# Turning the softmax tiles of a two-layer encoder: sixteen SBUF-to-SBUF transfers in place of a trip through DRAM

## The chip, the cores and the metric

The kernel runs on one core of a Trainium2 chip. The metric is the device time of one execution in microseconds (us), the median of several runs. A profiled execution is one more run, with every instruction recorded.

## The reference

Two transformer layers over 256 rows of 2048 numbers in float32, 16 heads of 128.

```python
# layer 1
u = rms_norm(h, a_norm_g);  q, k, v, fz = split(u @ a_w_in)      # 2048 x (3*2048 + 16)
q, k = rms_norm per head
logf = log_sigmoid(fz + a_b_f);  c = cumsum(logf)
s = q k^T * scale + c[query] - c[key];  causal;  p = softmax(s);  o = p v
h = h + o @ a_w_out
h = h + (relu(rms_norm(h) @ w1) ** 2) @ w2                       # 2048 -> 8192 -> 2048
# shared keys and values, then layer 2
k, v = split(rms_norm(h, kv_norm_g) @ kv_w);  k = rms_norm per head
q = rms_norm per head of rms_norm(h, b_norm_g) @ b_w_q
s = q k^T * scale + bias by distance;  chunks of 64 see themselves and the 8 before;  p = softmax(s);  o = p v
h = h + o @ b_w_out
h = h + the same MLP with its own weights
```

What the change touches is p: for each of the 16 heads and both layers, the softmax probabilities have to be transposed (turned) before the product with v.

## The kernel before

All matrix products are made on TensorE to float32 accuracy from two rounded halves: a tile of weights is split into `hi` (ScalarE, L323) and `lo` (VectorE, L324), activations likewise, and three products hi*hi, hi*lo, lo*hi are summed in PSUM (L592, L594, L596). Many weight blocks also go through a scheme of seven products in place of eight, for which sums of weight blocks are needed (T1 to T4); `make` (L970) forms them on VectorE, and `put` (L980) by a transfer from POOL's queue that adds to its destination. Tiles named `raw`, `zraw`, `R`, `w`, `wT`, `wB` are weights: loaded by `load` (L299) or `bring` (L942) on SP's queue, with four `raw` buffers.

Between two weight tiles `run_fill` works off one or two steps of a list, `fill`; `add_fill` puts small work there, numbered by step. So the attention of one group of four heads runs in between the weight products of the next: `attend` places, from a table, the four steps of `softmax` for each head, then the transfers that turn the probabilities, and some steps later `values` (the product with v, L766 and L767). The order on TensorE, VectorE, ScalarE and SP's queue is the order in which the code is written (`keep_order`); on POOL it is kept for computing alone, and its transfers are placed by the scheduler.

A tile of probabilities, 128 queries by 384 (128 keys for the first 128 queries, 256 for the second), is turned in two moves. VectorE transposes each 32x32 block where it stands (`blocks32`, L440, from `pr` to `z`). Then the blocks must change places: block row i and block column j swap. Both helpers below do that second move. `carry` writes the tile to DRAM whole (`rows`, L450) and, one step later, reads it back in four transfers that take the columns (`columns`, L456). `hop` sends each of the sixteen blocks of 32 partitions straight from SBUF to SBUF (L466): eight from SP's queue, eight from POOL's. In the kernel before, `hop` serves some tiles of the MLP (`turn_hidden`, where a table entry is negative; 32 x 256 numbers a block) and `carry` all others. `z`, `pr` and `pT` of the softmax are slices of one buffer, `pbuf`, so the profile calls all three `pbuf`. There are three rooms for z and four for pT.

POOL also takes the power -0.5 for the norms of the heads (`norm`, L668), for which ScalarE (L674) waits, and prepares the attention's bias (L912 to L917, L1243, L1245).

Of the kernel before, what the change touches and what calls it, by code (L numbers as in the profile page):

```python
# [99 lines left out]
def trunk(ctx: ExitStack, tc: tile.TileContext, xT, xr, gs, hg, bf, wgate, w_in, w_oa, w1a, w1fa, w1sa, w2fa, w2sa,  # L100
# [336 lines left out]
    def blocks32(src, z, b):  # L437
        n = src.shape[1] // P
        nb = z.shape[1] // (n * P)
        V.transpose(z.rearrange("p (j n b c) -> p b n j c", j=4, n=n, b=nb)[:, b],  # L440
                    src.rearrange("p (n j c) -> p n j c", n=n, j=4))

    def carry(z, dst, wait=1, reader=SY):
        w = z.shape[1]
        n = w // 4
        box = []

        def rows():
            box.append(dram.tile([P, w], F32, name="turn", tag=f"turn{w}", bufs=4))
            SY.dma_start(box[0], z)  # L450

        def columns():
            s = box[0].rearrange("(i a) f -> a i f", i=4)
            d = dst.rearrange("p (i f) -> p i f", i=4)
            for j in range(4):
                reader.dma_start(d[32 * j : 32 * j + 32], s[:, :, j * n : (j + 1) * n])  # L456

        return [[rows]] + [[]] * wait + [[columns], [], []]

    def hop(z, dst):  # L460
        n = z.shape[1] // 4

        def go():
            for i in range(4):
                for j in range(4):
                    (G if i % 2 else SY).dma_start(dst[32 * j : 32 * j + 32, i * n : (i + 1) * n], z[32 * i : 32 * i + 32, j * n : (j + 1) * n])  # L466

        return [[go], [], [], [], []]
# [257 lines left out]
    def softmax(st, g, a, q, k, bias, cq):  # L726
        s = ps_o.tile([P, 512], F32, name="po", tag="po")
        TE.matmul(s[:, 0:P], q[:, a, 0:P], k[:, a, 0], start=True, stop=True)  # L728
        TE.matmul(s[:, P : 3 * P], q[:, a, P:T], k[:, a], start=True, stop=True)  # L729
        yield  # L730
        t = wk.tile([P, 3 * P], F32, name="t", tag="wk")
        pr = rooms("pr")
        row = sm.tile([P, 3 * NB], F32, name="row")
        nm, su, rs = (row[:, i * NB : i * NB + NB] for i in range(3))
        halves = ((0, slice(0, P)), (1, slice(P, 3 * P)))
        for b, c in halves:
            if cq is not None:
                V.scalar_tensor_tensor(t[:, c], s[:, c], cq[:, b, g * GH + a : g * GH + a + 1], bias[:, a, c],
                                       op0=ALU.add, op1=ALU.add)
                V.tensor_reduce(nm[:, b : b + 1], t[:, c], axis=AX.X, op=ALU.max, negate=True)  # L740
            else:
                V.tensor_tensor_reduce(out=t[:, c], in0=s[:, c], in1=bias[:, a, c], scale=-1.0, scalar=-3.0 * NEG,
                                       op0=ALU.add, op1=ALU.min, accum_out=nm[:, b : b + 1])
        yield
        for b, c in halves:
            S.activation(pr[:, c], t[:, c], AF.Exp, bias=nm[:, b : b + 1], scale=1.0 if cq is not None else -1.0,
                         accum_out=su[:, b : b + 1])
        yield
        V.reciprocal(rs, su)
        for b, c in halves:  # L750
            V.tensor_scalar(pr[:, c], pr[:, c], rs[:, b : b + 1], None, op0=ALU.mult)
        z = rooms("z")
        blocks32(pr, z, 0)
        st["pT"] = rooms("pT")
        st["carry"] = carry(z, st["pT"], 0)
        yield

    served = set()
# [14 lines left out]
    def attend(g, q, k, v, cq, o, make_bias):  # L773
        st = [{} for _ in range(GH)]
        box = {}
        k4 = k.rearrange("p (i a b c) -> p a b i c", i=4, a=GH, b=NB)
        *at, far = TABLES["ATA" if cq else "ATB"][g]
        items = [[] for _ in range(at[-1] + far + 1)]
        step = steps(lambda: make_bias(g, box))
        for i in (5, 8, 9) if cq and g == 0 else (3, 6, 7):  # L780
            items[i].append(step)
        for a in range(GH):
            step = steps(lambda a=a: softmax(st[a], g, a, q(), k4, box["b"], cq() if cq else None))
            for i in range(4):
                items[at[a] + i].append(step)
            items[at[a] + 3].append(lambda a=a: add_fill(st[a]["carry"]))
            items[at[a] + far].append(lambda a=a: values(st[a], a, v, o, g * GH + a))
        return items
# [589 lines left out]
```

## Time and profile before

| what | before |
|---|---|
| median of three runs | 2051.86 us (2051.32 to 2054.9) |
| profiled execution | 2049.66 us, span 2047.9 us |
| TensorE busy | 2041.1 us |
| VectorE, ScalarE, POOL busy | 1783.5, 1403.7, 245.0 us |
| bytes moved by DMA | 557.78 MB, 272 GB/s |
| granted TensorE clock | 0.999 |

The span runs from the first instruction to the last. PE is TensorE, PEld its weight loads, DVE VectorE, ACT ScalarE, SP the engine that only issues transfers. A time behind an engine is the union of its instructions' times. `out<-in` names the tiles that an instruction writes and reads, L and a number the line of the kernel.

### The profile page before, as it was taken

To read this page: it belongs to the slowest core of one execution; us is meant where nothing else is said; L and a number is where in the kernel's file an instruction comes from. 1 tells how busy PE (TensorE), PEld (TensorE's weight loads), DVE (VectorE), ACT (ScalarE), POOL (GpSimd) and SP (SyncE) were. 2 spreads that over 40 slices of the span, in tenths; PEclk is the share of its full clock that TensorE was granted. 3 is DMA by queue.
4 is the path that set the end of the run, shared out by engine and by line. 5 is a ranking of instruction groups with operands and counts; after the bars stand their busy time and mean duration, and the time that the engine had idled before them with its cause. 6 is when DMAs were issued, how large, how long until landed. Compare 5 with 4: busy or idle time off the path is not lost.

```text
span 2047.9 us, 27097 instructions
## 1 busy us (share of the span) xinstructions
PE 2041.1 (100%) x9062; PEld 1688.5 (82%) x9062; DVE 1783.5 (87%) x2065; ACT 1403.7 (69%) x1805; POOL 245.0 (12%) x351
## 2 busy tenths in 40 slices
PE   9999999999999999999999999999999999999999
PEld 7888888888888888888888888888888888888887
DVE  7788888998898899899988778888988998988996
ACT  7766666677677677677778666667766676776764
POOL 1111110011111102101012111001101111111020
PEclk9999999999999999999999999999999999999999
DMA  8898888998888898898879888888988888888984
GB/s 322 265 298 272 266 280 243 309 278 272 282 262 281 272 293 272 247 292 273 260 242 311 275 254 287 255 264 284 291 291 265 266 270 284 266 284 261 299 259 147
DMA packets 175309, 557.78 MB, mean 272 GB/s; under 512 B 40624, under 2 KB 69184, under 8 KB 152640
## 3 DMA queue, kind: packets, MB, share of 16 engines
q1 hardware_dynamic: 154112, 464.99, 63.9%
q0 software_dynamic: 20768, 90.75, 22.5%
q8 instruction: 71, 1.16, 0.2%
q14 instruction: 70, 0.57, 0.1%
q10 hardware_dynamic: 288, 0.30, 0.1%
HBM read 516.07 MB, written 27.29 MB: 265 GB/s over the span
## 4 chain that ended last, share of the span: by engine, by line
PE 98%; DVE 1%; ACT 1%; issue 0%; DMA 0%; DVEq 0%; ACTq 0%
PE acc L596 23%; PE acc L592 23%; PE acc L594 23%; PE s L592 9%; PE s L594 9%; PE s L596 9%; PE po L729 1%; PE po L766 1%; DVE lo L324 0%; PE po L767 0%; PE po L728 0%; ACT hi L323 0%; DMA gsb<-in_gs 0%; PE pg L868 0%; DVE s L995 0%
## 5 line engine op out<-in xcount | busy, mean ns | idle before, releaser
L324 DVE TENSOR_TENSOR lo<-raw,hi 128x1024 fp32r<-128x1024 f32 (+1 forms) x409 | 493.5, 1211 | 81.5 <-ACT hi L323 77.1
L323 ACT ACTIVATE hi<-raw 128x1024 fp32r<-128x1024 f32 (+1 forms) x409 | 429.5, 1054 | 194.0 <-PE acc L594 123.4
L592 PE MATMUL acc<-hi,act 128*128 128x512 f32 x1774 | 496.3, 393 | 0.7 <-ACT hi L323 0.7
L596 PE MATMUL acc<-lo,act 128*128 128x512 f32 x1774 | 491.1, 390 | 0.7 <-DVE lo L324 0.6
L594 PE MATMUL acc<-hi,act 128*128 128x512 f32 x1774 | 490.7, 389 | 0.0
L596 PEld LDWEIGHTS acc<-lo,act 128*128 128x128 f32 x1774 | 332.5, 188 | 72.1 <-DVE lo L324 3.1
L594 PEld LDWEIGHTS acc<-hi,act 128*128 128x128 f32 x1774 | 333.0, 188 | 70.1 <-DVE act L383 0.5
L592 PEld LDWEIGHTS acc<-hi,act 128*128 128x128 f32 x1774 | 331.2, 188 | 69.6 <-ACT hi L323 2.1
L323 ACT ACTIVATE hi<-w 128x1024 fp32r<-128x1024 f32 x254 | 267.0, 1058 | 124.0 <-PE acc L594 82.7
L324 DVE TENSOR_TENSOR lo<-wT,hi 128x1024 fp32r<-128x1024 f32 x220 | 267.2, 1221 | 66.1 <-ACT hi L323 62.2
L324 DVE TENSOR_TENSOR lo<-w,hi 128x1024 fp32r<-128x1024 f32 x254 | 305.3, 1217 | 14.0 <-ACT hi L323 12.3
L323 ACT ACTIVATE hi<-wT 128x1024 fp32r<-128x1024 f32 x220 | 232.1, 1059 | 102.1 <-PE acc L594 48.5
L592 PE MATMUL s<-hi,act 128*128 128x512 f32 x530 | 146.3, 391 | 0.0
L596 PE MATMUL s<-lo,act 128*128 128x512 f32 x530 | 145.0, 389 | 0.0
L594 PE MATMUL s<-hi,act 128*128 128x512 f32 x530 | 144.8, 388 | 0.0
L466 POOL DMA_DIRECT2D q<-z x192 | 95.7, 510 | 255.1 <-DVE z L440 211.0
L596 PEld LDWEIGHTS s<-lo,act 128*128 128x128 f32 x530 | 99.2, 188 | 20.8 <-DVE lo L324 0.5
L594 PEld LDWEIGHTS s<-hi,act 128*128 128x128 f32 x530 | 99.4, 188 | 20.6
L592 PEld LDWEIGHTS s<-hi,act 128*128 128x128 f32 x530 | 99.1, 188 | 20.2
L592 PE MATMUL s<-hi,S 128*128 128x512 f32 x288 | 89.6, 392 | 0.0
L596 PE MATMUL s<-lo,S 128*128 128x512 f32 x288 | 88.8, 390 | 0.0
L594 PE MATMUL s<-hi,S 128*128 128x512 f32 x288 | 88.7, 389 | 0.0
(217 smaller groups left out, 2284.4 us busy)
## 6 DMA issues: line engine op xcount, KB each, us to landing
raw<-in_w_in SPq DMA_DIRECT2D x75, 512.0 KB, 5.9
w<-in_w2fa SPq DMA_DIRECT2D x32, 1024.0 KB, 6.5
w<-in_w2fb SPq DMA_DIRECT2D x32, 1024.0 KB, 6.2
w<-in_w1fa SPq DMA_DIRECT2D x27, 1024.0 KB, 7.0
w<-in_w1fb SPq DMA_DIRECT2D x27, 1024.0 KB, 7.3
raw<-in_w2sa SPq DMA_DIRECT2D x52, 512.0 KB, 7.0
raw<-in_w2sb SPq DMA_DIRECT2D x50, 512.0 KB, 7.3
raw<-in_w_kv SPq DMA_DIRECT2D x48, 512.0 KB, 5.1
```

The source lines that it names most:

```text
L323: S.activation(hi[:, c], raw[:, c], AF.Copy)
L324: V.tensor_tensor(lo[:, c], raw[:, c], hi[:, c].bitcast(F32), op=ALU.subtract)
L466: (G if i % 2 else SY).dma_start(dst[32 * j : 32 * j + 32, i * n : (i + 1) * n], z[32 * i : 32 * i + 32, j * n : (j + 1) * n])
L592: TE.matmul(ps[:, cols], xh, cut(hi, j), start=first, stop=False, **kw)
L594: TE.matmul(ps[:, cols], xl, cut(hi, j), start=False, stop=False, **kw)
L596: TE.matmul(ps[:, cols], xh, cut(lo, j), start=False, stop=last, **kw)
L729: TE.matmul(s[:, P : 3 * P], q[:, a, P:T], k[:, a], start=True, stop=True)
L766: TE.matmul(po[:, :T], v[:, 0, a * P : (a + 1) * P], pT[:, :2], start=True, stop=False)
```

## The change

The softmax step hands its tile to `hop` in place of `carry`. `[:4]` cuts the list of steps to the length that `carry` gave, so that `values` keeps its step. The sixteen transfers are issued in the step in which the DRAM write was; there is no second step.

```diff
         z = rooms("z")
         blocks32(pr, z, 0)
         st["pT"] = rooms("pT")
-        st["carry"] = carry(z, st["pT"], 0)
+        st["carry"] = hop(z, st["pT"])[:4]
         yield
```

Nothing moves on TensorE, VectorE and ScalarE. On SP the change is seen best at the end of the first attention, where the tiles come in pairs. SP before (`x8` stands for eight rows alike; L299 and L942 load weights):

```order
L299 DMA raw<-in_w_oa 128x1024
L450 DMA turn<-pbuf 128x384 x2
L299 DMA raw<-in_w_oa 128x1024
L456 DMA pbuf<-turn 32x4x96 x8
L299 DMA raw<-in_w_oa 128x1024
L450 DMA turn<-pbuf 128x384 x2
L942 DMA w_3022<-in_w1a 128x1024
L456 DMA pbuf<-turn 32x4x96 x8
L299 DMA raw<-in_w_oa 128x1024 x3
```

SP now, at the same place:

```order
L299 DMA raw<-in_w_oa 128x1024
L466 DMA pbuf<-pbuf 32x96 x16
L299 DMA raw<-in_w_oa 128x1024 x2
L466 DMA pbuf<-pbuf 32x96 x16
L942 DMA w_3190<-in_w1a 128x1024
L299 DMA raw<-in_w_oa 128x1024 x3
```

The two weight loads that stood among the old transfers now stand together between two bursts of sixteen, and the load of w comes behind the second burst.

POOL's queue at that place before: the bias of the last group, the norm, then the accumulating transfers alone.

```order
L912 DMA nb<-cd 128x1536
L668 TENSOR_TENSOR ss<-ss,mhalf 128x4 x2
L914 AFFINE_SELECT nb<-nb 128x4x128
L917 AFFINE_SELECT nb<-nb 128x4x128
L980 DMA wT_2419<-in_w_oa 128x1024
L980 DMA wB<-in_w_oa 128x1024
L980 DMA wT_2927<-in_w_oa 128x1024
```

POOL's queue now:

```order
L912 DMA nb<-cd 128x1536
L668 TENSOR_TENSOR ss<-ss,mhalf 128x4 x2
L914 AFFINE_SELECT nb<-nb 128x4x128
L917 AFFINE_SELECT nb<-nb 128x4x128
L466 DMA pbuf<-pbuf 32x96 x8
L980 DMA wT_2509<-in_w_oa 128x1024
L466 DMA pbuf<-pbuf 32x96 x16
L980 DMA wB<-in_w_oa 128x1024
L466 DMA pbuf<-pbuf 32x96 x16
L980 DMA wT_3075<-in_w_oa 128x1024
```

Bursts of eight for one tile, or sixteen for two, now stand between the accumulating transfers. Near the start of the attention the same happens around the norm. POOL before:

```order
L980 DMA R<-in_w_in 128x1024
L980 DMA wT_843<-in_w_in 128x1024
L668 TENSOR_TENSOR ss<-ss,mhalf 128x4 x2
L912 DMA nb<-cd 128x1536
L980 DMA R<-in_w_in 128x1024
```

POOL now:

```order
L980 DMA R<-in_w_in 128x1024
L466 DMA pbuf<-pbuf 32x96 x8
L980 DMA wT_843<-in_w_in 128x1024
L466 DMA pbuf<-pbuf 32x96 x8
L668 TENSOR_TENSOR ss<-ss,mhalf 128x4 x2
L466 DMA pbuf<-pbuf 32x96 x8
L912 DMA nb<-cd 128x1536
```

The second tile's eight transfers stand ahead of the norm's power on POOL.

## The prediction

> **What bounds the kernel.** First the page: the busy line and the chain that ended last. Then the waits of TensorE alone.
>
> ```profile
> span 2047.9 us, 27097 instructions
> ...
> PE 2041.1 (100%) x9062; PEld 1688.5 (82%) x9062; DVE 1783.5 (87%) x2065; ACT 1403.7 (69%) x1805; POOL 245.0 (12%) x351
> ...
> PE 98%; DVE 1%; ACT 1%; issue 0%; DMA 0%; DVEq 0%; ACTq 0%
> ...
> L324 DVE TENSOR_TENSOR lo<-raw,hi 128x1024 fp32r<-128x1024 f32 (+1 forms) x409 | 493.5, 1211 | 81.5 <-ACT hi L323 77.1
> ```
>
> ```profile
> PE pt L141 <- DVE mhalf L143: 1.0, 1, 1.0
> PE acc L592 <- ACT hi L323: 0.7, 1, 0.7
> PE acc L596 <- DVE lo L324: 0.6, 1, 0.6
> ```
>
> TensorE is busy for 2041.1 of 2047.9 us and carries 98% of the chain. Its waits add up to 2.3 us and none of them ends on a softmax tile. So the trip through DRAM, however long, is hidden today, and the reader should look for one thing only: whether something that TensorE needs now comes later than TensorE asks for it. Three things can: the turned tile itself (read by L766), the weights behind it in SP's queue, and the work behind it in POOL's queue.
>
> **What an edit costs on its queue.** The rows of the old way, then those of the same helper where the kernel already uses it (`hop` on the MLP's tiles, 1024 bytes a row against 384 here).
>
> ```profile
> L456 SPq DMA_DIRECT2D pbuf<-turn x128: 302/430/1470, 97.8 to 1330.7; - x128
> ...
> L450 SPq DMA_DIRECT2D turn<-pbuf x32: 319/332/522, 95.9 to 1323.6; - x32
> ...
> DMA to landing us min/median/max: 1.8/3.4/8.0
> ```
>
> ```profile
> L466 SPq DMA_DIRECT2D q<-z x192: 507/589/1777, 407.4 to 1978.2; - x192
> L466 POOL DMA_DIRECT2D q<-z x192: 496/503/554, 408.0 to 1977.9; - x192
> ...
> DMA to landing us min/median/max: 1.7/4.7/7.5
> ```
>
> Removed per tile: 0.33 + 4 x 0.43 = 2.1 us of issuing on SP, and SP's wait between the two steps. Added: 8 x 0.589 = 4.7 us on SP and 8 x 0.503 = 4.0 us on POOL. For 32 tiles that is 83 us more on SP and 129 us more on POOL, which works for 245.0 us now. A burst of eight that nothing holds up, and one that is held up:
>
> ```profile
> 1809.34 4.95 SPq L466 DMA_DIRECT2D q<-z  x8
> ```
>
> ```profile
> 1809.60 3.95 POOL L466 DMA_DIRECT2D q<-z  x8 [6.19 <-DVE z L440]
> ```
>
> ```profile
> 407.97 3.51 POOL L466 DMA_DIRECT2D q<-z  x7 [3.00 <-DMA raw<-in_w1sa]
> 414.40 0.50 POOL L466 DMA_DIRECT2D q<-z  x1 [2.92 <-DMA w<-in_w1fa]
> ```
>
> ```profile
> 407.41 7.15 SPq L466 DMA_DIRECT2D q<-z  x8
> ```
>
> The wait of 2.92 us is for the weight sum issued eight transfers earlier on POOL. The program counts each queue's transfers on eight semaphores in turn, so every transfer waits until the eighth before it has landed. A burst of eight thus takes 4.95 us on SP when the eight before it have landed, and 7.15 us behind late ones.
>
> **The tightest place: two tiles at once, at 310 us.** At the end of each attention the softmax tiles come in pairs. These are the fourth pair's turns on VectorE, SP's queue around it, the product that reads the second tile, and how long the old column reads took to land there (1.8 to 3.4 us) and the weight load of 306.99 us (6.5 us).
>
> ```profile
> 309.51 0.58 DVE L440 STREAM_TRANSPOSE pbuf<-pbuf 128x384 f32<-128x384 f32 x1
> ...
> 310.76 0.58 DVE L440 STREAM_TRANSPOSE pbuf<-pbuf 128x384 f32<-128x384 f32 x1
> ```
>
> ```profile
> 299.10 1.77 SPq L450 DMA_DIRECT2D turn<-pbuf  x2
> ...
> 306.99 0.39 SPq L299 DMA_DIRECT2D raw<-in_w_oa  x1
> 310.12 1.57 SPq L450 DMA_DIRECT2D turn<-pbuf  x2
> ```
>
> ```profile
> 320.95 0.60 PE L766 MATMUL po<-pbuf,R 128*128 128x256 f32 x2
> ```
>
> ```profile
> DMA to landing us min/median/max: 1.8/2.4/3.4
> ```
>
> ```profile
> DMA to landing us min/median/max: 6.5/6.5/6.5
> ```
>
> The tiles are ready at 310.1 and 311.3; the product stands in TensorE's order at 320.95 us, 9.6 us after the second turn. Now both bursts go through SP one after the other: from 310.12, sixteen issues of 0.589 us with their gaps, 2 x 4.95 = 9.9 us, so the last is issued at about 319.5 and lands 2.4 us later, at 321.9. That is 1.0 us late. Before it comes the pair of 299.1, whose sixteen issues hold SP until 309.0 instead of 306.5, so that the two weight loads behind them go out together at about 309.2. By the eight semaphores the seventh and eighth transfer of the new pair wait for those loads; with 6.5 us they land by 315.8, while SP reaches the seventh at 313.7. So up to 2.1 us more; I take half, 1.0. **Term: 2.0 us**, straight on the path, since TensorE takes its products in written order. Its ends: 0 (columns' shortest landing of 1.8 and no wait gives 0.4 late, which the next stage may have in hand) and 5.5 (below, second rival). POOL has eight of each sixteen transfers at 0.503 us and is done sooner.
>
> The Trainium skill (DMA: Bandwidth & Descriptors, "Anatomy of one DMA") puts a DMA at about 2.0 us plus bytes over 436 GB/s, which by that page would be an estimate of 2.03 us for 12 KB; with it in place of 2.4 the term would be 1.6 us. No run here shows a transfer of this size.
>
> **The next tightest places.** The last pair of the second attention, and the tightest single tile:
>
> ```profile
> 1321.78 0.58 DVE L440 STREAM_TRANSPOSE pbuf<-pbuf 128x384 f32<-128x384 f32 x1
> ...
> 1323.02 0.58 DVE L440 STREAM_TRANSPOSE pbuf<-pbuf 128x384 f32<-128x384 f32 x1
> ```
>
> ```profile
> 1337.18 0.60 PE L766 MATMUL po<-pbuf,R 128*128 128x256 f32 x2
> ```
>
> ```profile
> 270.76 0.58 DVE L440 STREAM_TRANSPOSE pbuf<-pbuf 128x384 f32<-128x384 f32 x1
> ```
>
> ```profile
> 281.54 0.59 PE L766 MATMUL po<-pbuf,R 128*128 128x256 f32 x2
> ```
>
> The pair: 1322.4 + 9.9 - 0.5 + 2.4 = 1334.2 against 1337.18, 3 us to spare. The single tile: 271.34 + 4.95 - 0.5 + 2.4 = 278.2 against 281.54, 3.3 us to spare on SP. **Term: 0.3 us** for both, between 0 and the 2.7 us of the second rival. The other 28 tiles, read the same way between the first and the last rows of these two groups, have 11.7 us (the first tile) or more from the turn's end to the product:
>
> ```profile
> L766 PE MATMUL po<-pbuf,R x64: 376/377/382, 107.5 to 1337.4; 128*128 128x256 f32 x64
> ...
> L440 DVE STREAM_TRANSPOSE pbuf<-pbuf x32: 578/578/582, 95.3 to 1323.0; 128x384 f32<-128x384 f32 x32
> ```
>
> **POOL's queue.** POOL also takes the power for the head norms (L668), and ScalarE waits for it. The tile of 103.9 us comes just ahead of one:
>
> ```profile
> 103.30 0.58 DVE L440 STREAM_TRANSPOSE pbuf<-pbuf 128x384 f32<-128x384 f32 x1
> ```
>
> ```profile
> 107.47 2.77 POOL L668 TENSOR_TENSOR ss<-ss,mhalf 128x4 f32<-128x4 f32 x2 [7.48 <-DVE ss L667]
> ```
>
> ```profile
> 108.54 1.14 ACT L674 ACTIVATE qn<-s,ss 128x128 f32<-128x128 f32 x4 [0.70 <-POOL ss L668]
> ```
>
> Eight issues from 103.88 end at 107.9, or up to 0.5 later behind a landing, so the power starts 0.4 to 0.9 us late, and ScalarE already waits for it there. What of this reaches TensorE depends on how far the split weights (hi, lo) stand ahead. **Term: 0.3 us**, from 0 to 0.9. The accumulating transfers of POOL (L980) move by as little where a burst comes ahead of them.
>
> **SP's weight loads.** Each tile holds them up by 4.95 - 2.1 = 2.9 us, a pair by about 6, less what SP no longer waits for:
>
> ```profile
> SPq L456 <- DMA turn<-pbuf: 32.7, 20, 3.5
> ```
>
> ```profile
> ACT hi L323 <- PE acc L594: 290.1, 354, 2.6
> ```
>
> The 32.7 us of 20 waits go away, 1.6 us each. The cover is that ScalarE, which splits a weight tile into hi and lo, mostly waits for TensorE to free a buffer (354 times) rather than for a load: the loads are early. A late one first eats that; with the cover gone it would cost what the load is late. **Term: 0**, up to 2 us. **Gain of the shorter trip: 0**: TensorE waits for no softmax tile, and 1.0 of the 2.3 us above lies in the warm-up at the start; at most 1.3 us.
>
> **Sum.** 2.0 + 0.3 + 0.3 + 0 + 0 = 2.6 us. The profiled execution took 2049.66 us around its span of 2047.9, 2.2 us under the median of 2051.86. Set on the median: 2051.86 + 2.6 = 2054.5 us, 0.13% more. A measurement of this kernel tells about 0.2% (4.1 us) from no change, so I forecast no change that shows.
>
> **Rivals.**
> 1. All of it is hidden: the narrow transfers land as fast as the shortest ones and the weight loads ahead are early. For it: 0.4 us late at the tightest place, in the best case. Time 2051.9 us, give or take 1.
> 2. Slower, by the eight semaphores. If the first burst of a pair is held up as that of 407.41 was (7.15 us) and transfers land in the 4.7 us median of the wide ones, the last transfer of the pair at 310 us lands at 310.12 + 7.15 + 4.4 + 4.7 = 326.4, 5.5 us late; that of the second attention at 1322.4 + 7.15 + 4.4 + 4.7 = 1338.7, 1.5 late; the single tile at 271.34 + 7.15 - 0.6 + 4.7 = 282.6, 1.1 late. With POOL's 0.3 that is 8.4 us: 2060.3 us. It decides from a landing of about 3.7 us with one held-up burst on (4.5 us late at 310). For it: the wide transfers' median. Against it: the old narrow reads landed in 2.4 us at that very place.
> 3. POOL is kept from building its transfers while VectorE works. If each issue waited for one lo (1.211 us, first fence), sixteen would take 16 x 1.71 = 27.4 us: the pairs would land at 339.9 and 1352.2, 19 and 15 us late, some 34 us in all, 2086 us. Against it: 3.95 us for eight, with VectorE busy for 87% of the span.
>    The Trainium skill (SBUF — State Buffer, "SBUF: two separate sides") says that VectorE's two-port operations lock GpSimd out of writing descriptors. By that rule this rival would be near; the trace's 0.503 us median with a maximum of 0.554 does not agree with it for the operations that run here.
> 4. Faster: without the trip SP is free 1.6 us sooner at 20 places and less goes through the DMA queues. That needs a TensorE wait to remove; 2.3 us are there, so at the utmost 2049.6 us.
>
> **Chances.** Forecast (late at 310 us alone, 1 to 4 us in all) 0.45; rival 1 0.21; rival 2 0.23; rival 3 0.04; rival 4 0.05; weight loads late beyond their cover 0.02. Slower by over 0.2%: rivals 2 and 3, the loads, and 0.03 of the forecast's upper end: 0.32. Faster by over 0.2%: at most 0.04, from rival 4 and the scatter of the runs. The same: 0.64. The range goes from 2050.7 us (rival 1 and half of rival 4) to 2060.3 us (rival 2).
>
> **What would show it.** Right: in TensorE's waits, one new line, L766 waiting for a DMA pbuf<-pbuf by 1 to 4 us at 321 us and none elsewhere; SP's sixteen issues in 10 to 12 us; POOL busy for some 375 us; the DMA's bytes lower. Wrong: no such line (rival 1), several of them at 281 and 1337 us (rival 2), POOL issues over 0.6 us (rival 3), or TensorE waiting for hi and lo after the pairs, which would mean that the weights' cover was thinner than I read it.

## The result: slower by 1.1%

The changed kernel takes 2076.93 us (median of four runs, 2069.56 to 2078.5) against 2051.99 us for the kernel before beside it: 1.0112 times as long, with a 95% interval from 1.0085 to 1.0138. The prediction was 2054.5 us with a range to 2060.3, so it was wrong: 25 us are lost where 2.6, too little to be told, were forecast. The profiled execution took 2075.81 us. Its page, the span, the busy line and the chain:

```profile
span 2074.0 us, 27778 instructions
...
PE 2051.6 (99%) x9062; PEld 1689.1 (81%) x9062; DVE 1784.1 (86%) x2065; ACT 1403.4 (68%) x1805; POOL 373.5 (18%) x607
...
PE 86%; DMA 7%; DVE 2%; ACT 2%; SPq 1%; issue 1%; POOL 0%; DVEq 0%; ACTq 0%; POOLq 0%
```

TensorE had 98% of the chain before; now DMA has 7% of it. TensorE's waits (total us, times, longest):

```profile
PE po L728 <- DMA R<-turn: 8.9, 4, 3.4
PE acc L592 <- ACT act L770: 1.8, 1, 1.8
PE acc L592 <- ACT hi L323: 1.8, 3, 0.7
PE po L766 <- DMA pbuf<-pbuf: 1.5, 2, 1.2
PE acc L596 <- DVE lo L324: 1.3, 3, 0.6
```

The first line is the one to look at. It is not the softmax tile (L766, 1.5 us) but the scores q k (L728), which wait for `R<-turn`: the turned keys. The keys, too, are turned through DRAM by `carry`, with one write (L450, `turn<-z`) and four reads (L456, `R<-turn`), all from SP's queue, and the change had left them as they were.

**How it comes about, at one place.** SP's queue around the fourth group of keys (the last of the first attention), first before:

```profile
274.90 0.33 SPq L450 DMA_DIRECT2D turn<-z  x1
276.38 1.78 SPq L456 DMA_DIRECT2D pbuf<-turn  x4
278.21 0.43 SPq L299 DMA_DIRECT2D raw<-in_w_oa  x1
280.13 1.73 SPq L456 DMA_DIRECT2D R<-turn  x4
```

and the scores that read these keys, in TensorE's rows, with no wait:

```profile
287.66 0.38 PE L728 MATMUL po<-R,q 128*128 128x128 f32 x2
```

VectorE had turned the keys' blocks just before, from 274.17 us on:

```profile
274.17 0.70 DVE L440 STREAM_TRANSPOSE z<-qn 128x512 f32<-128x512 f32 x1
```

SP wrote them 0.03 us after that ended, and the last read was issued at 281.86, 5.8 us ahead of the scores. Now the same after, VectorE's row, SP's queue and TensorE's row:

```profile
279.62 0.71 DVE L440 STREAM_TRANSPOSE z<-qn 128x512 f32<-128x512 f32 x1
```

```profile
276.88 5.18 SPq L466 DMA_DIRECT2D pbuf<-pbuf  x8
282.10 0.58 SPq L942 DMA_DIRECT2D R<-in_w_oa  x1
282.79 0.37 SPq L299 DMA_DIRECT2D raw<-in_w_oa  x1
283.25 0.38 SPq L450 DMA_DIRECT2D turn<-z  x1
283.72 0.38 SPq L299 DMA_DIRECT2D raw<-in_w_oa  x1
289.69 2.16 SPq L456 DMA_DIRECT2D R<-turn  x4
```

```profile
296.27 0.46 PE L728 MATMUL po<-R,q 128*128 128x128 f32 x2 [3.38 <-DMA R<-turn]
```

The keys' blocks are ready at 280.33 us, but SP is in the burst of eight until 282.06 and sends two weight loads that had queued up behind it; the keys' write goes out at 283.25, 2.9 us late. The four reads wait for its landing and start 6.4 us behind it (5.2 before); the last is issued at 291.85 and lands at 296.13, and TensorE has stood still for 3.38 us when it starts at 296.27. From the landing of the keys to the scores there were, over the eight groups of keys, 1.04 to 11.54 us in the kernel before. Four groups now come late: the two with the least in hand, 1.04 us (scores of 1298.48) and 2.43 us (287.66), but also two that had 6.18 us (223.76) and 8.08 us (1255.67). At the last of these, both steps of the keys' turn stand behind a burst after the change:

```profile
1250.00 5.64 SPq L466 DMA_DIRECT2D pbuf<-pbuf  x7
1255.75 0.52 SPq L450 DMA_DIRECT2D turn<-z  x1
1256.37 0.38 SPq L299 DMA_DIRECT2D raw<-in_w_kv  x1
1256.85 5.46 SPq L466 DMA_DIRECT2D pbuf<-pbuf  x8
1262.34 2.02 SPq L456 DMA_DIRECT2D R<-turn  x4
```

The keys' blocks are ready at 1250.04 us, so the write goes out 5.7 us late; it has landed at 1259.63, and the reads start 2.7 us after that. At the scores of 223.76 it is different again: SP sends the write at once, but it takes 8.1 us to land where it took 3.1. Five weight loads that a burst of 9.41 us had held up went out just ahead of it; no run shows whether they are the reason.

**Where the 25 us are.** TensorE executes the same instructions in the same order in both kernels, so the starts can be subtracted one by one. Of the 26.1 us between the two spans, 10.0 arise from 90 to 345 us (first attention), 12.3 from 1165 to 1345 us (second), 2.5 between them and 1.8 behind, while 0.5 us are gained ahead of 90 us. The steps:

| what TensorE does there (start before) | us lost |
|---|---|
| scores L728 wait for the keys (223.76, 287.66, 1255.67, 1298.48) | 0.80 + 3.54 + 3.20 + 2.03 = 9.6 |
| products at a lower clock right behind two of these | 2.8 |
| weights and activations late behind a pair's bursts (1340.61, 1347.41) | 1.96 + 0.99 = 3.0 |
| softmax tile, L766 (320.95, 1337.18) | 0.46 + 1.32 = 1.8 |
| behind POOL's power (111.56) | 0.9 |
| steps under 0.8 us each | 8.0 |

The second row shows in TensorE's clock, in three stretches: behind the stalls of 1270.9 and 1317.5 us and, for comparison, behind that of 296.2 us (columns: window, its length, PE's busy time and matmuls, granted clock, DMA's share, GB/s):

```profile
1270.80:1274.00 3.20, 3.08 (x8) 0.51 1.03 411
1317.50:1321.80 4.30, 4.24 (x14) 0.64 0.95 209
296.20:300.00 3.80, 3.73 (x19) 1.00 1.02 410
```

The third row is SP behind the last pair of the second attention, and what ScalarE waits for there:

```profile
1345.78 11.63 SPq L466 DMA_DIRECT2D pbuf<-pbuf  x16
```

```profile
1362.84 1.06 ACT L323 ACTIVATE hi<-raw 128x1024 fp32r<-128x1024 f32 x1 [4.72 <-DMA raw<-in_w_ob]
```

Sixteen transfers hold SP for 11.63 us; the weight load behind them is 4.72 us late for ScalarE, whose other work (`act`, which TensorE needs) waits behind that one.

### The profile page after: what moved, and what is told of

The parts are those of the page before. It is cut to its first block, busy times and chain, and to the rows that moved or that the text cites. A ratio compares the mean times of both kernels' runs of the same rounds, so it can differ in the third digit from the quotient of the medians.

```text
span 2074.0 us, 27778 instructions
## 1 busy us (share of the span) xinstructions
PE 2051.6 (99%) x9062; PEld 1689.1 (81%) x9062; DVE 1784.1 (86%) x2065; ACT 1403.4 (68%) x1805; POOL 373.5 (18%) x607
## 4 chain that ended last, share of the span: by engine, by line
PE 86%; DMA 7%; DVE 2%; ACT 2%; SPq 1%; issue 1%; POOL 0%; DVEq 0%; ACTq 0%; POOLq 0%
PE acc L592 20%; PE acc L596 20%; PE acc L594 20%; PE s L592 8%; PE s L596 8%; PE s L594 8%; DVE lo L324 1%; DMA turn<-z 1%; DMA R<-turn 1%; DMA pbuf<-pbuf 1%; SPq L466 1%; DMA raw<-in_w_kv 1%; ACT hi L323 1%; DMA q<-turn 1%; DMA z<-turn 1%
## 5 line engine op out<-in xcount | busy, mean ns | idle before, releaser
L592 PE MATMUL acc<-hi,act 128*128 128x512 f32 x1774 | 498.0, 394 | 3.9 <-ACT act L770 1.8
L596 PE MATMUL acc<-lo,act 128*128 128x512 f32 x1774 | 491.7, 390 | 1.4 <-DVE lo L324 1.3
L596 PEld LDWEIGHTS acc<-lo,act 128*128 128x128 f32 x1774 | 332.1, 188 | 74.6 <-DVE lo L324 5.9
L592 PEld LDWEIGHTS acc<-hi,act 128*128 128x128 f32 x1774 | 331.4, 188 | 75.1 <-ACT hi L323 5.6
L466 POOL DMA_DIRECT2D pbuf<-pbuf x256 | 127.9, 516 | 177.0 <-issue 54.6
L592 PE MATMUL s<-hi,act 128*128 128x512 f32 x530 | 146.9, 392 | 0.1
L596 PE MATMUL s<-lo,act 128*128 128x512 f32 x530 | 145.4, 390 | 0.3 <-DVE lo L324 0.3
L596 PEld LDWEIGHTS s<-lo,act 128*128 128x128 f32 x530 | 99.5, 189 | 21.9 <-DVE lo L324 1.5
L592 PEld LDWEIGHTS s<-hi,act 128*128 128x128 f32 x530 | 99.1, 188 | 20.8 <-ACT hi L323 0.5
L592 PE MATMUL s<-hi,S 128*128 128x512 f32 x288 | 89.7, 393 | 0.8 <-DVE acc L1020 0.8
L596 PE MATMUL s<-lo,S 128*128 128x512 f32 x288 | 89.0, 390 | 0.2 <-DVE lo L324 0.2
```

Source lines behind the costliest of these rows:

```text
L592: TE.matmul(ps[:, cols], xh, cut(hi, j), start=first, stop=False, **kw)
L596: TE.matmul(ps[:, cols], xh, cut(lo, j), start=False, stop=last, **kw)
```

## The experiments

Theory A: SP's queue. The bursts hold up what stands behind them, the keys' turn above all. Rivals: POOL's half; the transfers themselves, whoever issues them; something spread over the whole program. The kernel before ran beside each; its median was 2052.6 us in the first four and 2052.5 in the last four.

**e1_sp_load: SP's time alone.** The kernel before, with five more transfers of 32 x 96 numbers per softmax tile from SP into a part of `pbuf` that nothing reads.

```diff
+    def dead(z):
+        for k in range(5):
+            p, c = slice(32 * (k % 4), 32 * (k % 4) + 32), 9 * 3 * P + k // 4 * 96
+            SY.dma_start(rooms.t[p, c : c + 96], z[p, k % 4 * 96 : k % 4 * 96 + 96])
...
         st["carry"] = carry(z, st["pT"], 0)
+        st["carry"][0].append(lambda: dead(z))
```

> The kernel before (turning through DRAM), plus five extra 32x96 transfers per softmax tile on SP's queue that nothing reads, so that SP issues for about 4.8 us a tile as with the change (2.1 + 5 x 0.55). Theory A (SP's queue: its longer bursts push back the keys' turn and the weight loads behind them): TensorE waits at L728 for R<-turn return, and the time rises by 15 to 30 us. Theory B (the new path itself brings the turned tile late, or SBUF-to-SBUF traffic slows everything): within 4 us of before. Theory C (POOL's queue): within 4 us of before.

Measured: 2074.57 us (2073.44 to 2075.64), 1.0108 [1.0091, 1.0124]: as slow as the change. TensorE's waits (its L772 and L733 are L766 and L728 of the change):

```profile
PE po L772 <- DMA pbuf<-turn: 10.8, 3, 4.7
PE po L733 <- DMA R<-turn: 3.7, 2, 2.0
```

Every softmax tile still goes through DRAM and POOL has nothing new, yet a loss of that size is there. So time on SP's queue suffices for it. Here it is mostly the softmax tile's own trip through DRAM that comes late, since it stands behind the added transfers in the same queue; the keys come second.

**e2_pool_load: POOL's time alone.** The same with eight such transfers from POOL (`G` in place of `SY`, `range(8)`).

> The kernel before, plus eight extra 32x96 transfers per softmax tile on POOL's queue that nothing reads. Theory A (SP): within 4 us of before. Theory C (POOL's bursts delay the head norms' power and the accumulating transfers, and the 7 to 9 us of small steps come from there): 5 to 10 us slower.

Measured: 2055.85 us (2051.0 to 2060.98), 1.002 [1.0008, 1.0031]. The medians are 3.3 us apart, and the interval goes from 1.6 to 6.4 us. So POOL's time costs some 4 us, most likely less than theory C asked, though its lower end of 5 us is not excluded. ScalarE waits longer for POOL's power than the 7.4 us before:

```profile
ACT qn L674 <- POOL ss L668: 18.1, 13, 3.2
```

**e4_keys_too: the keys off the DRAM path.** The change, and `hop` for the keys as well.

```diff
-                turns = [[t] for _, _, _, t in rest] + carry(z, dst)
+                turns = [[t] for _, _, _, t in rest] + (away or carry)(z, dst)
...
-                    box.append(head_norm(lambda: st0, turned(), box[0]))
+                    box.append(head_norm(lambda: st0, turned(), box[0], away=hop))
```

> The change, with the turned keys of both attentions going SBUF to SBUF as well (32x256 blocks). Theory A, in its narrower form (what costs most is the keys' DRAM trip, whose two steps on SP end up behind the bursts): the waits at L728 for the keys shrink from 9 us to under 2, and with them the slow clock after the stalls; 8 to 12 us faster than the change. If SP's occupation as such is what counts (weights late), the eight more issues per key tile take that back: within 4 us of the change.

Measured: 2067.16 us (2065.75 to 2069.7), 1.0073 [1.0058, 1.0088]; the profiled span is 2064.0 us, 10.0 less than the change's. TensorE's waits:

```profile
PE po L766 <- DMA pbuf<-pbuf: 3.4, 1, 3.4
PE acc L592 <- ACT act L770: 2.0, 1, 2.0
PE acc L592 <- ACT hi L323: 1.8, 3, 0.7
```

The line of L728 is gone, although SP and POOL issue more transfers than in the change. The time falls by 9.8 us, within the 8 to 12 that theory A gave. So for this part of the loss it is not the load as such but what stands behind it: a write whose landing must be awaited, behind a burst. The other 14.6 us against the kernel before stay. They are spread: the pair at 320.95 us is now 3.4 us late, `act` of ScalarE 2.0 us, and the rest comes in smaller steps.

**e7_first_only: half the tiles.** The change in the first attention alone.

```diff
-        st["carry"] = hop(z, st["pT"])[:4]
+        st["carry"] = hop(z, st["pT"])[:4] if cq is not None else carry(z, st["pT"], 0)
```

> The hop in the first attention alone (16 of the 32 tiles); the second turns its softmax tiles through DRAM as before. Theory A, with the loss where the stalls stand: 10 to 13 us of it stay (90 to 345 us of the span) and the 12 us between 1165 and 1345 us go, so 2061 to 2066 us. Rival D, that the loss is spread over the whole program by another layout of code or a lower clock: 2070 us or more.

Measured: 2062.59 us (2060.69 to 2065.52), 1.0046 [1.0028, 1.0064]; of the span's 15.8 us more, 13.2 arise from 90 to 345 us and 0.0 from 1165 to 1345 us. The loss is where the bursts are, and rival D falls. The largest line of TensorE's waits is again the keys':

```profile
PE po L728 <- DMA R<-turn: 3.6, 2, 3.4
```

**e3_pool_only and e6_sp_only: all sixteen from one queue.** A loop like `hop`'s, with one queue (line numbers are 10 higher behind it):

```diff
+    def hop_on(z, dst, pick):
+        n = z.shape[1] // 4
+
+        def go():
+            for i in range(4):
+                for j in range(4):
+                    pick(i).dma_start(dst[32 * j : 32 * j + 32, i * n : (i + 1) * n], z[32 * i : 32 * i + 32, j * n : (j + 1) * n])
+
+        return [[go], [], [], []]
...
-        st["carry"] = hop(z, st["pT"])[:4]
+        st["carry"] = hop_on(z, st["pT"], lambda i: SY)      # e3: lambda i: G
```

> The change with all sixteen transfers of a tile on POOL's queue and none on SP's. Theory A: the waits at L728 go away; what is left is POOL's sixteen issues of 0.5 us (8 us a tile, 16 a pair), so only L766 of the pairs waits (8 to 12 us in all): 5 to 15 us slower than before, 10 to 20 faster than the change. Theory C: slower than the change.

> The change with all sixteen transfers of a tile issued by SP (9.4 us of SP's queue per tile instead of 4.7, none on POOL). Theory A: SP's added time goes from about 83 us to 234 us, and keys and weights behind it come 5 us later again at each tile: 2100 to 2200 us, L728's waits for R<-turn over 20 us in all. Rival C, that POOL's half matters as much as SP's, so that moving it away gives time back: 2060 to 2090 us.

Measured: POOL alone 2156.61 us (2153.84 to 2159.37), 1.0507 [1.049, 1.0524]; SP alone 2202.8 us (2201.28 to 2206.56), 1.0735 [1.0717, 1.0753]. TensorE's waits with POOL alone:

```profile
PE po L776 <- DMA pbuf<-pbuf: 42.2, 11, 8.3
PE acc L602 <- ACT hi L323: 19.2, 6, 7.2
PE s L602 <- ACT hi L323: 9.3, 1, 9.3
```

and with SP alone:

```profile
PE po L776 <- DMA pbuf<-pbuf: 41.1, 9, 8.5
PE acc L602 <- ACT hi L323: 28.7, 9, 7.1
PE po L738 <- DMA R<-turn: 24.7, 3, 12.7
```

Sixteen from SP alone cost 150 us, where eight from each queue cost 25; sixteen from POOL alone cost 104, where eight cost 4 in e2, in which, however, nothing waited for what they carried. The waits are not all of it: TensorE's busy time is also 29.8 us (POOL) and 40.5 us (SP) longer than before, at a granted clock of 0.981 and 0.972. SP came out as theory A said (over 20 us for the keys, the time just above the upper end). POOL did not: I had expected waits at the pairs alone, and with sixteen the softmax tile itself is late eleven times. The time is what theory C foretold, slower than the change. So POOL's queue is no free place either, though with eight transfers a tile e2 puts it at some 4 us. A queue's price is small until its slack is used up, and rises steeply then.

**e5_act_half: SP's half from ScalarE.** `pick` is `lambda i: G if i % 2 else S`.

> The change with the half of the hop that SP issued issued by ScalarE instead (8 transfers per tile on ScalarE's queue, 8 on POOL's, none on SP's). Theory A, that the loss came from SP's queue (eight 0.59 us issues per tile ahead of the keys' turn and of the weights): the waits of the scores (L728) for R<-turn fall from 8.9 us to under 1 us, and the loss of 25 us falls to 0 to 14 us (2052 to 2066 us), of which 4 us are POOL's half and the rest what ScalarE, 68% busy, pays for 256 issues. Theory B, that the 512 narrow transfers themselves or their arrival cost the time, whichever queue issues them: 2070 us or more, with L728 still waiting 5 us or more.

Measured: 2179.26 us (2177.15 to 2181.72), 1.0618 [1.0601, 1.0635]. No wait of L728 and none of the tile over 0.3 us is left, so sixteen narrow transfers a tile are not late by themselves, and theory B's own mark is missing. TensorE's waits alone would be weak evidence, since TensorE was held up elsewhere and so asked for keys and tiles later. But from the end of its turn on VectorE to its landing a tile took 8.8 us in the median, against 9.3 in the kernel before and 10.1 in the change, and that does not depend on when TensorE asks. The time I gave for theory A, at most 2066 us, is missed by over 110 us. TensorE waits for ScalarE:

```profile
PE acc L602 <- ACT hi L323: 38.1, 14, 6.5
PE s L602 <- ACT hi L323: 36.9, 13, 7.5
```

ScalarE's rows at one burst show why:

```profile
194.93 7.76 ACTq L476 DMA_DIRECT2D pbuf<-pbuf  x8
202.73 1.14 ACT L684 ACTIVATE qn<-acc,ss 128x128 f32<-128x128 f32 x4 [7.63 <-DMA pbuf<-pbuf]
```

While it issues, ScalarE does not calculate: here 7.76 us for eight transfers in which no weight tile is split. This is the longest of the 32 bursts; most take 5 to 6 us. All issues together:

```profile
L476 ACTq DMA_DIRECT2D pbuf<-pbuf x256: 513/602/1484, 97.3 to 1455.1; - x128
```

256 x 0.602 = 154 us of ScalarE, placed in the two attentions, where TensorE leaves no such gap. I had set that price at 10 us at most because ScalarE works for only 68% of the span; that is an average, and not a gap of 5 to 8 us at these places.

**e8_paced: the same transfers, four in each of four steps.** In one of the 32 tiles the order of the program lets the last two of the four groups carry values of a later tile, whose turn has by then taken the same room, so that tile's product is not the reference's. The transfers are the same in number and size.

```diff
+    def paced(z, dst):
+        n = z.shape[1] // 4
+
+        def go(j):
+            for i in range(4):
+                (G if i % 2 else SY).dma_start(dst[32 * j : 32 * j + 32, i * n : (i + 1) * n], z[32 * i : 32 * i + 32, j * n : (j + 1) * n])
+
+        return [[lambda j=j: go(j)] for j in range(4)]
...
-        st["carry"] = hop(z, st["pT"])[:4]
+        st["carry"] = paced(z, st["pT"])
```

> The change with the same sixteen transfers on the same two queues, but four of them (two on SP, two on POOL) in each of four successive steps instead of sixteen in one. Theory A1, that it is the burst which stands ahead of the keys' turn: L728's waits for R<-turn fall from 8.9 us to under 3 us, and 5 to 12 us of the loss come back (2064 to 2072 us), less 0 to 4 us for the last columns, which are issued three steps later. Theory A2, that it is SP's time in all, however it is spread: 2072 to 2082 us, L728's waits as in the change.

Measured: 2084.63 us (2079.59 to 2085.75), 1.0152 [1.0133, 1.017]. TensorE's waits (L737 is L728, L775 is L766):

```profile
PE po L775 <- DMA pbuf<-pbuf: 23.8, 8, 7.1
PE po L737 <- DMA R<-turn: 1.6, 1, 1.6
```

The keys' wait falls from 8.9 to 1.6 us, as A1 said. The time is nevertheless longer, above the range of either theory, since the tiles themselves now come late eight times; I had allowed 0 to 4 us for that and it was 23.8. Since TensorE is later here too, the wait alone does not show that the burst mattered; the keys' own trip does.

**The keys' trip.** From the end of the keys' turn on VectorE to the landing of their last read, in us, for the four groups that came late in the change (named by their scores' start before):

| scores | before | the change | e1 (SP's time) | e2 (POOL's time) | e5 (ScalarE for SP) | e8 (paced) |
|---|---|---|---|---|---|---|
| 223.76 | 10.5 | 16.6 | 15.2 | 10.7 | 12.3 | 12.4 |
| 287.66 | 10.4 | 15.8 | 18.5 | 9.8 | 10.9 | 10.5 |
| 1255.67 | 10.2 | 20.6 | 20.3 | 10.9 | 10.4 | 11.9 |
| 1298.48 | 13.0 | 14.8 | 13.0 | 14.0 | 14.7 | 14.4 |

The first three trips grow by 5 to 10 us with bursts on SP, whatever these carry, and by at most 2 us without SP's half or with SP's time in all unchanged but the burst broken up. So it is the burst on SP that makes these keys late. The fourth trip is much the same everywhere; that group came late because it had 1.04 us in hand.

The doses side by side (transfers of a softmax tile per queue; e1's 5 come on top of the 5 of the DRAM path):

| kernel | SP | POOL | ScalarE | us |
|---|---|---|---|---|
| before | 5 | 0 | 0 | 2052.0 to 2052.6 |
| e2 | 5 | 8, read by nothing | 0 | 2055.85 |
| e1 | 5 + 5, read by nothing | 0 | 0 | 2074.57 |
| the change | 8 | 8 | 0 | 2076.93 |
| e3 | 0 | 16 | 0 | 2156.61 |
| e5 | 0 | 8 | 8 | 2179.26 |
| e6 | 16 | 0 | 0 | 2202.8 |

None of them beats the kernel before, and none points to one that would: TensorE had 2.3 us of waits to give back.

## Why the prediction was wrong, by its steps

**The list of three things that can come late** is the step that failed. It named the turned tile, "the weights behind it in SP's queue" and "the work behind it in POOL's queue". SP's queue holds a fourth thing, the keys' own turn through DRAM, and it is the worst to delay, because its reads wait for its write to land. The term **SP's weight loads: 0, up to 2 us** was thus put on the wrong rows. I asked only for the cover of the weights. One look at what L728 reads, and how long ahead it had landed, would have shown covers of 1.04 and 2.43 us, under my 2.9 us a tile, and with them two of the four late groups (5.6 of the 9.6 us). The other two had 6.18 and 8.08 us in hand and came late because their trips grew by 6.0 and 10.4 us, for which a delay of 2.9 was too small. That the keys' write of 283.25 is 2.9 us late is partly luck: 1.7 us are the rest of a burst, 1.2 us the two weight loads ahead. The step is shown by e4 (the waits go when the keys leave the path), e8 (the trips shorten when the burst is broken) and e1 (SP's time alone lengthens them). The keys' waits and the slow clock behind them are 9.6 + 2.8 = 12.4 of the 26 us.

**The weights themselves** were not free either: 3.0 us behind the last pair, and probably most of the 8 us in small steps. Nearly all of these steps stand at products that read a newly split weight tile (L592, L596), and ScalarE waits 25.5 us for `raw<-in_w_in` where it waited 4.7. No run separates those small steps from POOL's part, so that share stays open.

**The tightest place, 2.0 us at 320.95:** the right place and the right mechanism; 0.46 us were lost there in the change.

```profile
316.99 11.78 SPq L466 DMA_DIRECT2D pbuf<-pbuf  x16
```

From the end of the first turn the second tile took 13.0 us to land, where my terms give 12.8. Two of them were off and cancelled, which was luck: the sixteen issues took 11.8 us, not 10.9, and the last landed in 1.75 us, not 2.4 (the 512 transfers of this size, 1.6 to 9.2, median 3.6). In the kernel before, the product stood 10.9 us behind that turn, so by these figures the pair alone would have been 2.1 us late. It lost less because the keys' stalls had made TensorE later and VectorE not as much. With the keys' waits gone (e4) the pair was 3.4 us late, there with the keys' transfers in the same queues.

**The next tightest, 0.3 us:** the pair of 1337.18 was 1.32 us late, within its 2.7; 281.54 was not late.

**POOL's queue, 0.3 us, up to 0.9:** the power's delay showed at 111.56 us with 0.9 us. POOL's whole load of 4 us (e2) is above the bound. POOL was busy for 373.5 us, where some 375 were forecast.

**The costs of the issues** held: in the change's rows, SP and POOL (min/median/max in ns):

```profile
L466 SPq DMA_DIRECT2D pbuf<-pbuf x256: 507/588/1491, 95.4 to 1356.8; - x128
L466 POOL DMA_DIRECT2D pbuf<-pbuf x256: 496/498/887, 95.7 to 1355.5; - x128
```

588 and 498 ns against 589 and 503 taken from the wide transfers. So **rival 3** (POOL held off by VectorE) has nothing for it; 8 of the 256 POOL issues took more than its 0.6 us, at most 0.887. **Rival 2** gave a time on the right side, but by L766 at 310, 1322 and 281 us, and these lost 1.8 us together. **Rivals 1 and 4** are out: nothing was gained on the way, since no wait stood there.

**What would show it wrong** named TensorE waiting for hi and lo behind the pairs; it did, with little. The line that came first, L728, was not on that list.

## What to carry to other kernels

Before work is added to a queue, list everything that stands behind it there, and for each the time from its landing to its reader; the smallest is what the queue can give, however idle the queue is on average. A chain of dependent transfers (write, wait, read) in that queue can be held up at each of its steps, as at 1255.67, and the delays add up. Engines that also calculate are no free place for issuing: eight issues took ScalarE 5 to 8 us.

## What the runs showed of the hardware

A stall costs more than its length. Behind the stall of 1270.9 us above, TensorE's products of 512 columns started 0.43 us apart for about 3 us, not 0.23, at a granted clock of 0.51; behind the one of 296.2 us, no shorter, the clock stayed at 1.00. I took all gaps of over 1.1 us between the starts of two matmuls in the traces of the nine kernels after, and looked at the granted clock within 3.5 us behind each. It fell to half behind 1 of 26 gaps under 2 us, 11 of 21 from 2 to 3 us, 16 of 19 from 3 to 4.1 us and all 33 longer ones. A drop, other than at the end of the program, lasts 3.4 us or a whole multiple of that, and the next thirty matmuls together took mostly 1.4 to 2.8 us longer. So, as an estimate from these counts, a stall of 3 us is to be counted as some 4.5.

The Trainium skill (TensorE: Matmul & The Clock Gate, "Part 1: The HAM clock gate") says that TensorE's clock falls to half after an idle window of about 3.4 us, and that these windows run freely. The traces agree on the half and on the chance by which equal stalls differ; they differ on the length, since 11 of 21 gaps of 2 to 3 us, shorter than such a window, were enough. Why is not shown.
